# Attention rows normalised by the product that transposes them

## The chip, the cores and the metric

The kernel runs on one core of a Trainium2 chip. The metric is the device time of one execution in microseconds (us). Before the change it is 1858.86 us, the median of three runs (1857.93 to 1861.39).

TensorE multiplies: `matmul(out, a, b)` writes aᵀ·b to PSUM, with `a` loaded as weights and `b` streamed through. VectorE, ScalarE and GpSimd work on tiles of 128 partitions, and SyncE issues most transfers.

## The reference, cut to what matters

The network is a two-layer block (a sparse attention, a gated linear attention, two MLPs), followed by a second block (attention, a two-way mLSTM, a gated FFN). All is in f32. Two of its parts take a softmax over keys and multiply the result by values:

```python
# layer A: 16 heads, 4 key heads, 512 tokens, causal, best 128 keys a query
logits = einsum('bqgrd,bqkgd->bqgrk', q_b, k_sel) * 64 ** -0.5
p = softmax(where(valid, logits, -inf), axis=-1)
o = einsum('bqgrk,bqkgd->bqgrd', p, v_sel)
...
# second block: 8 heads, 2 key heads, 512 tokens, no mask
s = einsum('bkgqd,bksd->bkgqs', q_blk, kt) * 64 ** -0.5
p = softmax(s, axis=-1)
o = einsum('bkgqs,bksd->bkgqd', p, vt)
```

## The kernel before, in words

Weights are cut into a high and a low part (type f32r) and each projection is made of three f32r products per block (`wh` by `xT_hi`, `wh` by `xT_lo`, `wl` by `xT_hi`); these are the rows named `ps_a` at line 77. Plain f32 products, not cut, are used in a few places: values of the attentions, the memory heads (lines 1241 and 1275), the gated linear attention (line 786 and others).

`softmax_pv` (line 410) does one block of 128 queries for eight heads. For each head:

1. Two f32r products give the scores in a PSUM bank of tag `s` (two banks). The queries carry a minus sign, so that the row minimum `mn` stands for the maximum.
2. VectorE takes the row minimum (line 428 with a mask, line 431 without).
3. ScalarE takes exp into `prob` and sums the row into `sum` (line 434).
4. VectorE takes the reciprocal `rcp` (line 436).
5. The tile `prob` is multiplied by `rcp` in place, on VectorE (line 438) or ScalarE (line 440), as a letter of `norm` says for each of the four heads of a group: `"dada"` in layer A, `"addd"` in the second block (`d` is VectorE, `a` is ScalarE).
6. TensorE transposes `prob` in pieces of 128 columns into a bank of tag `t` (two banks, line 443). The piece is the weights, the identity `net.ident` is streamed.
7. The bank is copied to `pt` (line 446 on VectorE, line 448 on ScalarE).

When four heads of a group are done, plain f32 products of values and `pt` follow (tag `o`).

Layer A calls it eight times: four query blocks with 1, 2, 3 and 4 key blocks of 128 (`W` = 128 to 512), and two groups of eight heads each. The second block calls it four times, always with `W` = 512. That is 96 heads and 288 transposes.

Around the attentions a list of steps (`ORDER_A`, `ORDER_2`) puts projections beside them, and a scheduler then sets the order on each engine by its own estimate of every instruction's cost, so that projection products stand between those of the attention. Each engine works through its own queue in order.

Of the kernel before, what the change touches and what calls it, by code (L numbers as in the profile page):

```python
# [10 lines left out]
F32 = mybir.dt.float32  # L11
F32R = mybir.dt.float32r
I32 = mybir.dt.int32
AF = mybir.ActivationFunctionType
ALU = mybir.AluOpType
# [11 lines left out]
P = 128  # L27
# [382 lines left out]
def softmax_pv(net, pool, t, W, nkb, qT, kTh, kTl, v, g0, bias, oh, ol, kofs, pw=512, norm="addd", copy="dddd"):  # L410

    nc = net.nc
    tsl = slice(t * P, (t + 1) * P)
    pso = net.bank("o")
    pts = []
    for gi in range(2):
        pt = pool.tile([P, NT, 4, P], F32, name="pt", bufs=2)
        for r in range(4):  # L420
            h = 4 * gi + r
            ps = net.bank("s")
            net.mm(ps[:, :W], qT[:, h, tsl], kTh[:, g0 + gi, :W], True, False)
            net.mm(ps[:, :W], qT[:, h, tsl], kTl[:, g0 + gi, :W], False, True)
            mn = pool.tile([P, 1], F32, name="mn", bufs=4)
            pr = pool.tile([P, pw], F32, tag="prob", name="prob", bufs=4)[:, :W]
            if bias is not None:
                nc.vector.tensor_tensor_reduce(pr, ps[:, :W], bias, 1.0, 3.0e38, ALU.add, ALU.min, mn)
                src = pr
            else:  # L430
                nc.vector.tensor_reduce(mn, ps[:, :W], axis=AX.X, op=ALU.min)
                src = ps[:, :W]
            sm = pool.tile([P, 1], F32, name="sum", bufs=4)
            nc.scalar.activation(pr, src, AF.Exp, bias=mn, scale=-1.0, accum_out=sm)  # L434
            rc = pool.tile([P, 1], F32, name="rcp", bufs=4)
            nc.vector.reciprocal(rc, sm)
            if norm[r] == "d":
                nc.vector.tensor_scalar(pr, pr, rc, None, op0=ALU.mult)
            else:
                nc.scalar.activation(pr, pr, AF.Copy, scale=rc)  # L440
            pst = net.bank("t")
            for kb in range(nkb):
                nc.tensor.transpose(pst[:, kb * P : (kb + 1) * P], pr[:, kb * P : (kb + 1) * P], net.ident)  # L443
            ptv = pst[:, :W].rearrange("p (k n) -> p k n", k=nkb)
            if copy[r] == "d":
                nc.vector.tensor_copy(pt[:, :nkb, r, :], ptv)
            else:
                nc.scalar.activation(pt[:, :nkb, r, :], ptv, AF.Copy)
        pts.append(pt)

    for kb in range(nkb):
        for gi in range(2):
            net.mm(pso[gi * 64 : gi * 64 + 64, :], v[:, kb, g0 + gi, :], pts[gi][:, kb].rearrange("p r n -> p (r n)"), kb == 0, kb == nkb - 1)
    net.split(oh[:, kofs : kofs + 4, tsl], ol[:, kofs : kofs + 4, tsl], pso.rearrange("p (r n) -> p r n", r=4))


def layer_a(net, first):
# [3 lines left out]
    with tc.tile_pool(name="da", bufs=1) as da:  # L461
# [8 lines left out]
        with tc.tile_pool(name="di", bufs=1) as di, tc.tile_pool(name="dr", bufs=2) as dr:  # L470
# [67 lines left out]
            def attend(t, gp):  # L538
                if gp == 0 and "oa" not in have:
                    have["oa"] = da.tile([P, 2, 4, S], F32R, tag="iq", name="oa")  # L540
                oh, ol = (have["oa"][:, 0], have["oa"][:, 1]) if gp == 0 else (net.xh, net.xl)
                softmax_pv(net, di, t, (t + 1) * P, t + 1, qT[gp], kTh, kTl, v, 2 * gp, bias[t], oh, ol, 4 * gp, 576, "dada", "aaaa")
# [462 lines left out]
def second(net):  # L1005
# [5 lines left out]
    with tc.tile_pool(name="sm", bufs=1) as sm:  # L1011
# [8 lines left out]
        with tc.tile_pool(name="sa", bufs=1) as sa:  # L1020
# [80 lines left out]
            with tc.tile_pool(name="sp2", bufs=1) as sp2:  # L1101
                run_steps(ORDER_2[1], flows, {"A": lambda t: softmax_pv(net, sp2, t, S, NT, qT, kTh, kTl, v, 0, None, oah, oal, 0)})
# [420 lines left out]
```

## Time and profile before

| what | value |
|---|---|
| median of three runs | 1858.86 us |
| profiled execution, its own time | 1859.66 us |
| its span, first to last instruction | 1857.9 us |
| mean granted TensorE clock | 0.993 |
| TensorE busy | 1815.5 us (98%) |
| VectorE busy | 1440.5 us (78%) |
| ScalarE busy | 912.3 us (49%) |
| TensorE products | 10564 |

PE is TensorE, PEld its weight loads, DVE is VectorE, ACT ScalarE, POOL GpSimd. Busy time is what an engine spent in instructions; several of TensorE's overlap, since products are pipelined, so the pace of a run of equal products is read from the run's length less one product's length, over their number less one. A granted clock of 1.00 is 2.4 GHz, one of 0.50 is 1.2 GHz. The chain of waits goes back from the last instruction to what released it at every step: only what stands on it sets the end.

### The profile page before, as it was taken

What the parts mean: (1) busy time and instruction counts of PE and PEld (TensorE: products, weight loads), DVE (VectorE), ACT (ScalarE), POOL (GpSimd) and SP (SyncE); (2) the same over time, 40 slices, a digit from 0 to 9 for tenths busy, and PEclk for the clock granted to TensorE, in tenths of its full rate; (3) what the DMA queues carried; (4) which work ended last, traced back from release to release, by engine and by line L of the source; (5) the groups of instructions that cost most, each with busy time, mean ns of one, the idle gap of its engine ahead of it and who ended that gap; (6) DMA issues with size and microseconds to landing.
All of it is one profiled execution on the core that took longest, in us unless ns stands there. A gap on an engine that the chain in (4) does not pass through costs nothing.

```text
span 1857.9 us, 26802 instructions
## 1 busy us (share of the span) xinstructions
PE 1815.5 (98%) x10564; PEld 1532.8 (83%) x10564; DVE 1440.5 (78%) x2467; ACT 912.3 (49%) x1600; POOL 19.0 (1%) x46
## 2 busy tenths in 40 slices
PE   8999999999999999999999999999999899999997
PEld 7865698988888888889888888777566689999996
DVE  5998589878678587468988777877876787788877
ACT  5568644444443544334544444445677445344334
POOL 0010000000000100000000000000000000000000
PEclk9999999999999999999999999999999999999999
DMA  4231244634324222126454323422112122333232
GB/s 143 91 68 52 67 139 158 207 117 148 103 91 134 61 69 69 68 91 188 140 180 140 113 92 111 139 73 81 46 41 69 45 91 68 114 114 114 79 104 91
DMA packets 127161, 190.80 MB, mean 103 GB/s; under 512 B 9279, under 2 KB 77835, under 8 KB 127036
## 3 DMA queue, kind: packets, MB, share of 16 engines
q1 hardware_dynamic: 126996, 189.03, 32.0%
q8 instruction: 83, 1.36, 0.3%
q14 instruction: 42, 0.34, 0.1%
q0 software_dynamic: 32, 0.07, 0.0%
q10 hardware_dynamic: 8, 0.00, 0.0%
HBM read 186.96 MB, written 2.12 MB: 102 GB/s over the span
## 4 chain that ended last, share of the span: by engine, by line
PE 92%; DVE 5%; ACT 2%; issue 0%; DMA 0%; POOL 0%; SPq 0%; DVEq 0%; ACTq 0%; POOLq 0%
PE ps_a L77 51%; PE ps_s L77 15%; PE ps_t L77 11%; PE ps_o L77 7%; PE ps_t L443 1%; PE ps_t L302 1%; PE ps_s L806 1%; PE ps_a L1275 1%; DVE wl L85 1%; PE ps_t L405 1%; PE ps_s L1241 1%; ACT prob L434 0%; PE ps_s L843 0%; PE ps_o L858 0%; ACT wh L88 0%
## 5 line engine op out<-in xcount | busy, mean ns | idle before, releaser
L88 ACT ACTIVATE wh<-wr 128x1024 fp32r<-128x1024 f32 (+2 forms) x284 | 258.6, 958 | 239.3 <-PE ps_t L77 113.3
L85 DVE TENSOR_TENSOR wl<-wr,wh 128x1024 fp32r<-128x1024 f32 (+2 forms) x284 | 304.1, 1104 | 84.6 <-ACT wh L88 55.1
L77 PE MATMUL ps_a<-wh,xT_hi 128*128 128x512 f32 (+3 forms) x536 | 205.3, 387 | 3.6 <-ACT xT_hi L88 2.2
L77 PE MATMUL ps_a<-wh,xT_lo 128*128 128x512 f32 (+3 forms) x536 | 204.3, 385 | 0.6 <-DVE xT_lo L85 0.6
L88 ACT ACTIVATE wsh<-wr 128x1024 fp32r<-128x1024 f32 x94 | 97.5, 1059 | 184.3 <-DVE wr L254 155.5
L77 PE MATMUL ps_a<-xT_hi,wh 128*128 128x256 f32 (+1 forms) x528 | 163.4, 321 | 0.9 <-DVE gtok L1097 0.5
L77 PE MATMUL ps_a<-xT_lo,wh 128*128 128x256 f32 (+1 forms) x528 | 162.7, 319 | 0.0
L77 PE MATMUL ps_a<-xT_hi,wl 128*128 128x256 f32 (+1 forms) x528 | 147.0, 319 | 0.0
L77 PE MATMUL ps_a<-wl,xT_hi 128*128 128x512 f32 (+3 forms) x536 | 143.6, 381 | 0.0
L77 PE MATMUL ps_s<-wh,hh 128*128 128x512 f32 x344 | 136.6, 397 | 0.1
L77 PE MATMUL ps_s<-wh,hl 128*128 128x512 f32 x344 | 136.7, 397 | 0.0
L77 PE MATMUL ps_a<-tl,wsh 128*128 128x256 f32 x528 | 132.1, 283 | 0.0
L77 PE MATMUL ps_a<-th,wsh 128*128 128x256 f32 x528 | 132.1, 282 | 0.0
L77 PEld LDWEIGHTS ps_a<-wh,xT_hi 128*128 128x128 f32 x536 | 101.5, 189 | 25.0 <-issue 4.5
L85 DVE TENSOR_TENSOR wsl<-wr,wsh 128x1024 fp32r<-128x1024 f32 x94 | 113.0, 1221 | 10.7 <-ACT wsh L88 10.7
L77 PEld LDWEIGHTS ps_a<-wh,xT_lo 128*128 128x128 f32 x536 | 101.5, 189 | 19.8 <-DVE xT_lo L85 1.4
L77 PE MATMUL ps_t<-wh,hl 128*128 128x512 f32 x296 | 117.4, 397 | 0.0
L77 PE MATMUL ps_t<-wh,hh 128*128 128x512 f32 x296 | 117.4, 396 | 0.0
L77 PEld LDWEIGHTS ps_a<-wl,xT_hi 128*128 128x128 f32 x536 | 95.6, 188 | 19.3 <-issue 1.6
L77 PEld LDWEIGHTS ps_a<-xT_hi,wh 128*128 128x128 f32 x528 | 100.1, 190 | 9.3 <-issue 0.8
L77 PEld LDWEIGHTS ps_a<-xT_lo,wh 128*128 128x128 f32 x528 | 100.0, 189 | 7.8 <-issue 0.8
L77 PEld LDWEIGHTS ps_a<-tl,wsh 128*128 128x128 f32 x528 | 100.3, 190 | 0.0
(437 smaller groups left out, 4122.3 us busy)
## 6 DMA issues: line engine op xcount, KB each, us to landing
wr<-in_mlp_w_up_dram SPq DMA_DIRECT2D x32, 1024.0 KB
wr<-in_mlp_w_down_dram SPq DMA_DIRECT2D x32, 1024.0 KB
mod_raw<-in_w_ada_dram SPq DMA_DIRECT2D x48, 512.0 KB
wr<-in_b_w_in_dram SPq DMA_DIRECT2D x12, 1024.0 KB
wr<-in_w_gate_dram SPq DMA_DIRECT2D x11, 1024.0 KB
wr<-in_w_up_dram SPq DMA_DIRECT2D x11, 1024.0 KB
wr<-in_w_in_dram SPq DMA_DIRECT2D x10, 1024.0 KB
wr<-in_w_down_dram SPq DMA_DIRECT2D x10, 1024.0 KB
```

The source lines that it names most:

```text
L77: self.nc.tensor.matmul(ps, lt, rt, start=first, stop=last)
L85: (eng or self.nc.vector).tensor_tensor(out, x, hi.bitcast(F32), op=ALU.subtract)
L88: self.nc.scalar.activation(out, x, AF.Copy)
L302: self.nc.tensor.transpose(ps[:, j * P : (j + 1) * P], src[:, j * P : (j + 1) * P], self.ident)
L405: nc.tensor.transpose(ps[:, j * P : (j + 1) * P], st[:, j0 + j, :], net.identr)
L443: nc.tensor.transpose(pst[:, kb * P : (kb + 1) * P], pr[:, kb * P : (kb + 1) * P], net.ident)
L806: nc.tensor.matmul(ps[:, c * 64 : c * 64 + 64], x[:, c * C : (c + 1) * C], xv[:, c * m : (c + 1) * m, 1, :], start=True, stop=True)
L1241: nc.tensor.matmul(ps, qk[:, 4 + h, a * P : (a + 1) * P], qk[:, h, :], start=True, stop=True)
L1275: nc.tensor.matmul(o, ws[a][:, b * P : (b + 1) * P], v1[:, a, h, 0:129], start=n == 0, stop=n == len(as_) - 1)
```

## The change

For each head a new tile `diag` of 128x128 is made: the identity, scaled row by row by `rcp`, on the engine that scaled `prob` before. `prob` stays unscaled. In place of the transposes stand matrix products of the same pieces of `prob` (weights) with `diag` (streamed), so that the result is probᵀ times the diagonal of reciprocal sums.

```diff
@@ -434,13 +434,15 @@
             nc.scalar.activation(pr, src, AF.Exp, bias=mn, scale=-1.0, accum_out=sm)
             rc = pool.tile([P, 1], F32, name="rcp", bufs=4)
             nc.vector.reciprocal(rc, sm)
+
+            dg = pool.tile([P, P], F32, name="diag", bufs=3)
             if norm[r] == "d":
-                nc.vector.tensor_scalar(pr, pr, rc, None, op0=ALU.mult)
+                nc.vector.tensor_scalar(dg, net.ident, rc, None, op0=ALU.mult)
             else:
-                nc.scalar.activation(pr, pr, AF.Copy, scale=rc)
+                nc.scalar.activation(dg, net.ident, AF.Copy, scale=rc)
             pst = net.bank("t")
             for kb in range(nkb):
-                nc.tensor.transpose(pst[:, kb * P : (kb + 1) * P], pr[:, kb * P : (kb + 1) * P], net.ident)
+                nc.tensor.matmul(pst[:, kb * P : (kb + 1) * P], pr[:, kb * P : (kb + 1) * P], dg, start=True, stop=True)
             ptv = pst[:, :W].rearrange("p (k n) -> p k n", k=nkb)
             if copy[r] == "d":
                 nc.vector.tensor_copy(pt[:, :nkb, r, :], ptv)
```

The scheduler sees other costs, and the order on the engines moves inside the two attentions. After the change the products of line 443 are at line 445.

TensorE, layer A, third query block of the second head group (`qT_171`, `W` = 384), before: scores `ps_s`, transposes `ps_t`, values `ps_o`, projection `ps_a`.

```order
L77 MATMUL ps_s<-kTh,qT_171 128x384
L77 MATMUL ps_s<-kTl,qT_171 128x384
L443 MATMUL ps_t<-ident,prob 128x128 x4
L77 MATMUL ps_s<-kTh,qT_171 128x384
L77 MATMUL ps_s<-kTl,qT_171 128x384
L77 MATMUL ps_o<-pt,v 64x512 x7
L443 MATMUL ps_t<-ident,prob 128x128 x6
L77 MATMUL ps_a<-wh,oa 128x512
L77 MATMUL ps_a<-wh,xT_hi 128x512
L443 MATMUL ps_t<-ident,prob 128x128 x6
```

The same place after the change:

```order
L77 MATMUL ps_a<-wh,oa 128x512 x3
L77 MATMUL ps_o<-pt,v 64x512 x7
L445 MATMUL ps_t<-diag,prob 128x128 x12
L77 MATMUL ps_s<-kTh,qT_171 128x384
L77 MATMUL ps_s<-kTl,qT_171 128x384
L77 MATMUL ps_s<-kTh,qT_171 128x384
L77 MATMUL ps_s<-kTl,qT_171 128x384
L77 MATMUL ps_o<-pt,v 64x512
L77 MATMUL ps_s<-kTh,qT_171 128x384
```

Twelve products to `ps_t` that stood in two runs of six, with projection products between, now stand in one, and three of the projection products stand ahead of them.

TensorE, second block, first query block (`aqT` are its queries), the difference; lines with - are of the kernel before, lines with + of the changed one.

```order
 L77 MATMUL ps_s<-akTh,aqT 128x512
 L77 MATMUL ps_s<-akTl,aqT 128x512
-L443 MATMUL ps_t<-ident,prob 128x128 x8
+L77 MATMUL ps_a<-xT_hi,wh 128x512
+L77 MATMUL ps_a<-xT_lo,wh 128x512
+L77 MATMUL ps_a<-xT_hi,wl 128x512
+L77 MATMUL ps_a<-xT_hi,wh 128x512
+L77 MATMUL ps_a<-xT_lo,wh 128x512
+L445 MATMUL ps_t<-diag,prob 128x128 x8
+L77 MATMUL ps_a<-xT_hi,wl 128x512
```

Here five projection products moved in ahead of the eight. Counted from the first to the last product to `ps_t` of an attention, projection products of 512 columns fall from 127 to 104 in layer A and from 119 to 104 in the second block. Outside the two attentions TensorE's order is the same, and so are the orders of SyncE's and GpSimd's queues.

## Rows read from the trace of the kernel before

**Rows 1.** The page: busy us (share of the span) xinstructions of each engine
```profile
span 1857.9 us, 26802 instructions
PE 1815.5 (98%) x10564; PEld 1532.8 (83%) x10564; DVE 1440.5 (78%) x2467; ACT 912.3 (49%) x1600; POOL 19.0 (1%) x46
```

**Rows 2.** Busy time by stretch: layer A's attention, between, second block's attention
```profile
core 0: us, PE busy (x) PEld busy (x) DVE busy (x) ACT busy (x) POOL busy (x), PEclk, DMA share, GB/s
...
105.00:216.00 111.00, 104.36 (x524) 67.58 (x524) 89.49 (x324) 94.32 (x259) 6.37 (x16) 1.00 0.18 48
216.00:1300.00 1084.00, 1076.00 (x6262) 928.93 (x6263) 831.78 (x1232) 479.07 (x727) 11.57 (x22) 1.00 0.37 117
1300.00:1386.00 86.00, 81.48 (x389) 55.04 (x389) 75.31 (x152) 60.64 (x107) 0.00 (x0) 0.98 0.15 37
```

**Rows 3.** Chain of waits, 105 to 216 us: shares by line
```profile
by line: PE ps_a L77 22.5%; PE ps_o L77 19.8%; PE ps_t L443 13.9%; PE ps_s L77 13.8%; ACT prob L434 6.4%; DVE prob L428 3.7%; ACT pt L448 3.0%; issue 2.1%; PE ps_t L405 1.9%; ACT prob L440 1.9%; DVE m L533 1.6%; ACT wh L88 1.3%; DVE sc L534
```

**Rows 4.** Chain of waits, 1300 to 1390 us: shares; pieces (start, us, what)
```profile
by line: PE ps_a L77 37.5%; PE ps_o L77 21.9%; PE ps_t L443 12.1%; PE ps_s L77 11.4%; DVE pt L446 5.6%; DVE mn L431 3.5%; DVE prob L438 2.7%; DVE wl L85 2.6%; ACT prob L434 1.8%; issue 0.7%; DVE rcp L436 0.5%
...
1318.50 3.58 PE ps_o L77 x14
...
1338.45 4.99 PE ps_o L77 x14
1359.68 2.33 PE ps_a L77 x10
```

**Rows 5.** Instructions of line 443: duration ns min/median/max, first and last start, forms
```profile
L443 PE MATMUL ps_t<-ident,prob x288: 270/272/332, 109.8 to 1384.1; 128*128 128x128 f32 x144
```

**Rows 6.** Timeline, second block: start us, us, engine, line, operation (one run of eight)
```profile
1306.25 1.03 PE L443 MATMUL ps_t<-ident,prob 128*128 128x128 f32 x8
```

**Rows 7.** Instructions of line 1275
```profile
L1275 PE MATMUL ps_a<-mv,wexp x160: 273/275/422, 1409.1 to 1460.2; 128*128 128x129 f32 x160
```

**Rows 8.** Instructions of lines 1241 and 786
```profile
L1241 PE MATMUL ps_s<-mqk x32: 590/592/697, 1399.9 to 1448.1; 128*128 128x512 f32 x32
...
L786 PE MATMUL ps_s<-ones,kq x32: 164/250/258, 655.4 to 710.0; 128*128 128x1 f32 x32
```

**Rows 9.** Timeline: runs of plain f32 products
```profile
655.41 0.95 PE L786 MATMUL ps_s<-ones,kq 128*128 128x1 f32 x8
...
1421.60 2.40 PE L1275 MATMUL ps_a<-mv,wexp 128*128 128x129 f32 x20
...
1437.05 1.02 PE L1241 MATMUL ps_s<-mqk 128*128 128x512 f32 x2
...
1456.10 0.71 PE L1275 MATMUL ps_a<-mv,wexp 128*128 128x129 f32 x4 [1.55 <-DVE wexp L1264]
```

**Rows 10.** Groups by shape, scalings: count, busy us, mean ns, idle before
```profile
L438 DVE TENSOR_SCALAR prob<-prob,rcp 128x512 f32<-128x512 f32 x32 | 15.1, 479 | 0.2
L438 DVE TENSOR_SCALAR prob<-prob,rcp 128x128 f32<-128x128 f32 x8 | 2.4, 304 | 0.0
...
L440 ACT ACTIVATE prob<-prob,rcp 128x512 f32<-128x512 f32 x16 | 11.5, 719 | 3.6 <-DVE rcp L436 3.5
L440 ACT ACTIVATE prob<-prob,rcp 128x128 f32<-128x128 f32 x8 | 3.2, 398 | 1.0 <-DVE rcp L436 1.0
```

**Rows 11.** Waits of TensorE, both attentions: us in total, times, longest
```profile
PE ps_s L77 <- DVE mn L428: 2.3, 6, 0.8
...
PE ps_s L77 <- ACT qT L407: 1.1, 1, 1.1
...
PE ps_t L443 <- DVE prob L438: 2.0, 2, 1.2
...
PE ps_s L77 <- ACT prob L434: 1.2, 3, 0.9
```

**Rows 12.** Busy time by stretch: the gap at 1334 us
```profile
1334.00:1338.00 4.00, 2.26 (x12) 1.24 (x11) 4.00 (x6) 3.09 (x5) 0.00 (x0) 0.97 0.00 0
1338.00:1342.00 4.00, 3.55 (x12) 1.12 (x13) 4.00 (x10) 2.06 (x5) 0.00 (x0) 0.60 0.70 181
```

## The prediction

> **What bounds the kernel now.** I read the engine shares first. TensorE is busy 98% of the span, VectorE 78%, ScalarE 49% [rows 1]. Then I cut the span at the two places where `softmax_pv` runs: attention of layer A at 105 to 216 us, attention of the second block at 1300 to 1386 us. In them TensorE is idle 111.00 - 104.36 = 6.64 us and 86.00 - 81.48 = 4.52 us, together 11.2 us; the long stretch between them has 8 us in 1084 [rows 2]. VectorE and ScalarE are not idle there (89 and 94 us of 111, 75 and 61 of 86), but neither is full. The chain of waits confirms it: in the first stretch the four TensorE products by name hold 22.5 + 19.8 + 13.9 + 13.8%, the transposes of line 443 alone 13.9%, while the scaling on ScalarE (line 440) holds 1.9%; in the second, transposes 12.1% and the scaling on VectorE (line 438) 2.7% [rows 3, 4]. So a microsecond put on TensorE here is a microsecond on the end, less what falls into those 11.2 us; a microsecond taken from the scaling is worth almost nothing.
>
> **The product in place of the transpose.** The change removes 288 transposes and adds 288 products of the same shape, 128 columns through 128x128 weights. The question is what a plain f32 product costs beside an f32 transpose. The trace has 288 transposes for the 288 that the code issues (8 heads x (1+2+3+4) blocks x 2 head groups, plus 8 heads x 4 x 4): one instruction each, 272 ns long and pipelined [rows 5]. Eight of them take 1.03 us, so one follows the other by (1.03 - 0.272) / 7 = 0.108 us [rows 6].
>
> The nearest plain f32 product is the memory head's `ws` by `v1`, 129 columns, line 1275. The code issues 80 of them (8 calls x 10), and the trace has 160; line 1241 issues 16, and the trace has 32 [rows 7, 8]. A plain f32 product is two instructions with a weight load each, a transpose is one. Twenty of them (ten products) take 2.40 us [rows 9]: (2.40 - 0.275) / 19 = 0.112 us each, 0.224 a product. Added per product: 0.224 - 0.108 = 0.115 us (from unrounded spacings 0.1118 and 0.1083); times 288: **33.2 us** of TensorE.
>
> No row shows this very product, so I bound it. Below: one-column f32 products, where only the weight load is left, follow each other by (0.95 - 0.250) / 7 = 0.100 us [rows 8, 9]; two of them less one transpose is 0.092, times 288 = 26.4 us. Above: four instructions alone with a wait ahead take 0.71 us [rows 9], (0.71 - 0.275) / 3 = 0.145; two less a transpose is 0.182, times 288 = 52.3 us. I take 33.2, since the x20 row has the shape of the new work to within a column and nearly all transposes stand in runs of four or eight.
>
> The trace also says why the price doubles: at 512 columns two instructions of line 1241 take 1.02 us [rows 9], (1.02 - 0.592 [rows 8]) = 0.43 us apart, four times the 0.108 us for four times the columns. An f32 instruction goes at one rate, transpose or not, and the product needs two.
>
> The Trainium skill speaks against this change: "Perfetto Trace Analysis", section Transposes, asks that a logical transpose use the transpose and not a standard matmul, because it skips the arithmetic. The rows agree in sign, with 0.108 against 0.224 us. It gives no figure; by it alone the sum would only be known to be above zero.
>
> **The scaling.** VectorE did 56 of the 96 scalings, ScalarE 40 (by the `norm` letters: 32 and 32 in layer A, 24 and 8 in the second block). Each now scales a 128x128 identity instead of a 128xW tile. On VectorE 128x512 takes 479 ns and 128x128 304; on ScalarE 719 and 398 [rows 10]. At most 56 x 0.175 = 9.8 us leaves VectorE and 40 x 0.321 = 12.8 us ScalarE (less in truth, since 64 of the scalings are layer A's and three quarters of those are narrower than 512). TensorE's work hides nearly all of it already. What lies on the chain is 1.9% of 111 = 2.1 us and 2.7% of 90 (the chain was read from 1300 to 1390) = 2.4 us [rows 3, 4]; cut in the ratio of the durations that is 2.1 x (1 - 398/719) + 2.4 x (1 - 304/479) = 0.9 + 0.9 = 1.8 us, which I count inside the idle term, not beside it.
>
> **The idle term.** TensorE waited for the row minimum, the scaling, the exp that frees a score bank, and new queries [rows 11]. With 288 products slower TensorE asks later for each of these, and the scaling comes sooner. The others set the pace less, so idle shrinks: below, nothing of it goes; above, all 11.2 us. I take half: **-5.6 us**. A dependent part is the clock. After the gap at 1334 to 1338 us (TensorE busy 2.26 of 4) the granted clock is 0.60 in the next 4 us, between the levels 1.2 and 2.4 GHz [rows 12], and fourteen `pt` products took 4.99 us, against 3.58 elsewhere [rows 4]. If the gap closes, 1.4 us come back; I take half, **-0.7 us**.
>
> **What the new order moves.** The planner knows that the product is longer and reorders both attentions; DMA and GpSimd queues keep their order, and so does TensorE outside the attentions. Between the first and the last transposing product there stand now 104 projection products of 512 columns where there were 127 (layer A), and 104 where there were 119 (second block). They are the work that covers the waits for exp. 38 fewer at 0.233 us (ten in 2.33 us [rows 4]) are 8.9 us of cover that now stands behind the attention. Cost between zero and 8.9 us of new idle; I take zero, because the longer products themselves (4 x 0.115 us more a head of width 512) give the other engines the same time. The new tile has three buffers, so a scaling waits until the products three heads back are done; queued behind it on its engine are the next minimum or exp. At a head every 86/32 = 2.7 us in the second block and 0.9 us of products a head I expect no wait; one that came would cost at most those 0.9 us.
>
> **Sum.** The profiled execution took 1859.66 us, 0.8 above the median 1858.86. 1859.66 + 33.2 - 5.6 - 0.7 = 1886.6, on the median's footing 1885.8; I say **1886 us**. All low ends together: 1858.9 + 26.4 - 11.2 - 1.4 = 1872.7. All high ends: 1858.9 + 52.3 + 8.9 = 1920.
>
> **Rivals.**
> Starved order: the cover that moved behind the attentions is missed, idle does not shrink but grows by 8.9: 1858.9 + 33.2 + 8.9 = 1901. For it: ScalarE is busy 94 us of 111 in layer A, and the new order puts twelve products and then three score pairs with little between them. Against: its own load falls. Chance 0.10.
> Absorbed: the product goes at the weight-load pace and all idle is filled, 1858.9 + 26.4 - 11.2 = 1874. For it: the spacing hardly depends on the columns below 129 (0.100 at one). Against: waits for `mn` and `qT` remain. Chance 0.07.
> Not slower: the two instructions of a product overlap as if one, so it costs what the transpose does, and the shorter scaling gives its 1.8 us back: 1857. It decides once a product stays under 0.108 + (11.2 + 1.8) / 288 = 0.153 us. For it: weight loads overlap products in the trace. Against: no plain f32 row is below 2 x 0.100. Chance 0.03. This is also the case in which the change does not do to TensorE what it says, a matrix product with all its passes.
> Four times: an f32 product costs four transposes: 4 x 0.108 = 0.433, so 0.325 x 288 = 93.6, 1952 us. Against: [rows 9] have the ratio at two. Chance 0.02. The Trainium skill has this rule: "TensorE: Matmul & The Clock Gate", section Terms, calls the transpose mode four times faster for FP32. The trace does not bear that ratio out at this size.
>
> **How the numbers follow.** The forecast, 1876 to 1897 with its own bounds, has 0.78. The range takes it whole but for its edges, with a little of Absorbed and of Starved: 1876 to 1898. A difference within 0.2% (3.7 us) is about what a measurement of this kernel cannot tell from none. Slower holds the forecast, Starved, Absorbed and Four times: 0.97; the 0.03 of Not slower I split 0.02 faster, 0.01 same.
>
> **What would show it.** In the profile after: line 445 with 576 instructions of about 275 ns, runs of eight products spaced 0.112 us; TensorE's busy time up by some 30 us and its count from 10564 to 10852; `diag` scalings of about 300 and 400 ns; idle in the two stretches under 11.2 us and granted clock near 1 there. Line 445 with 288 instructions, or runs at 0.14 us and more, would break the price; idle above 15 us the idle term; a change of the stretch between the attentions would mean something that I have not seen.

## The result

| | before | after |
|---|---|---|
| median | 1858.39 us (1856.33 to 1861.39) | 1879.68 us (1877.19 to 1881.01) |
| ratio, 95% interval | | 1.011, [1.0098, 1.0123] |
| profiled execution, its own time | 1859.66 us | 1879.21 us |
| span | 1857.9 us | 1877.4 us |

The change makes the kernel 21 us slower (18 to 23 by the interval). The forecast was 1886, 1876 to 1898.

The page of the changed kernel, its span and the busy time of each engine, stands against [rows 1]:

```profile
span 1877.4 us, 27426 instructions
PE 1843.6 (98%) x10852; PEld 1567.6 (83%) x10852; DVE 1436.0 (76%) x2467; ACT 907.0 (48%) x1600; POOL 18.9 (1%) x46
```

TensorE has the 288 more instructions that the text spoke of, and 28 us more busy time; VectorE and ScalarE together lost 10. The line of the product, as [rows 5]:

```profile
L445 PE MATMUL ps_t<-diag,prob x576: 270/275/377, 110.1 to 1399.0; 128*128 128x128 f32 x192
```

Two instructions a product, 275 ns long. Their pace, from the timeline of the second block, as [rows 6] and [rows 9]:

```profile
1316.33 1.95 PE L445 MATMUL ps_t<-diag,prob 128*128 128x128 f32 x16
```

(1.95 - 0.275) / 15 = 0.112 us, the figure taken for the sum. Now the stages. The view of busy time by stretch, cut at the same work in both kernels (first score product of layer A to the first product of the MLP's down projection; start of the gate transposes to the first memory head), before:

```profile
97.00:287.00 190.00, 183.21 (x978) 133.54 (x977) 151.47 (x424) 124.90 (x307) 6.37 (x16) 1.00 0.32 94
1284.20:1399.90 115.70, 111.00 (x518) 75.89 (x519) 93.82 (x186) 73.22 (x123) 2.29 (x12) 0.99 0.20 56
```

and after (columns as in [rows 2]), with the long stretch between the attentions in the middle:

```profile
97.38:298.10 200.72, 198.96 (x1138) 153.79 (x1136) 150.21 (x424) 122.17 (x307) 6.26 (x16) 1.00 0.31 90
226.00:1310.00 1084.00, 1076.32 (x6263) 929.94 (x6260) 831.62 (x1232) 478.59 (x726) 11.57 (x22) 1.00 0.37 118
1294.75:1418.78 124.03, 123.84 (x646) 91.19 (x647) 91.62 (x186) 70.82 (x123) 2.29 (x12) 1.00 0.18 51
```

The two stages are 10.7 and 8.3 us longer, and that is all but half a microsecond of the difference of the spans (19.5); between them, shifted by 10 us, 1084 us hold the same work as in [rows 2] (6263 products against 6262, busy 1076.32 us against 1076.00). TensorE's idle time in the stages goes from 6.79 + 4.70 = 11.5 us to 1.76 + 0.19 = 1.95. The granted clock of the second is 1.00 where it was 0.99. The chain of waits there, against [rows 4]:

```profile
by line: PE ps_a L77 34.7%; PE ps_t L445 31.2%; PE ps_o L77 19.1%; PE ps_s L77 15.1%
...
1331.10 3.58 PE ps_o L77 x14
...
1354.84 3.58 PE ps_o L77 x14
...
1381.49 3.58 PE ps_o L77 x14
...
1400.24 3.58 PE ps_o L77 x14
```

Nothing but TensorE is left on it: the copies, minima and scalings of VectorE that held 12% of it before are gone. All four runs of fourteen value products take 3.58 us; the one of 4.99 has gone with the gap ahead of it.

The scalings, against [rows 10] (groups by shape):

```profile
L440 DVE TENSOR_SCALAR diag<-ident,rcp 128x128 f32<-128x128 f32 x56 | 15.7, 283 | 0.6
L442 ACT ACTIVATE diag<-ident,rcp 128x128 f32<-128x128 f32 x40 | 15.7, 395 | 3.5 <-DVE rcp L436 3.2
```

And what TensorE waits for in layer A's attention, 105 to 226 us, against [rows 11]; in the second block the view is empty:

```profile
PE ps_t L405 <- DVE hst L395: 0.6, 1, 0.6
PE ps_t L445 <- DVE diag L440: 0.3, 1, 0.3
PE ps_o L77 <- ACT pt L450: 0.3, 1, 0.3
PE ps_s L77 <- DVE mn L428: 0.2, 1, 0.2
```

### The profile page after: what moved, and what is told of

It reads as the page before. It is cut to its first block, busy times and chain, and to the rows that moved or that the text cites. A ratio compares the mean times of both kernels' runs of the same rounds, so it can differ in the third digit from the quotient of the medians.

```text
span 1877.4 us, 27426 instructions
## 1 busy us (share of the span) xinstructions
PE 1843.6 (98%) x10852; PEld 1567.6 (83%) x10852; DVE 1436.0 (76%) x2467; ACT 907.0 (48%) x1600; POOL 18.9 (1%) x46
## 4 chain that ended last, share of the span: by engine, by line
PE 92%; DVE 5%; ACT 1%; DMA 1%; issue 0%; POOL 0%; SPq 0%; DVEq 0%; ACTq 0%; POOLq 0%
PE ps_a L77 50%; PE ps_s L77 15%; PE ps_t L77 11%; PE ps_o L77 7%; PE ps_t L445 3%; PE ps_t L302 1%; PE ps_s L808 1%; PE ps_a L1277 1%; DVE wl L85 1%; PE ps_t L405 1%; PE ps_s L1243 1%; PE ps_s L845 0%; DMA wr<-in_w_down_dram 0%; DVE sc L536 0%; PE ps_o L860 0%
## 5 line engine op out<-in xcount | busy, mean ns | idle before, releaser
L85 DVE TENSOR_TENSOR wsl<-wr,wsh 128x1024 fp32r<-128x1024 f32 x94 | 113.0, 1220 | 12.6 <-ACT wsh L88 12.6
L77 PEld LDWEIGHTS ps_a<-wh,xT_lo 128*128 128x128 f32 x536 | 101.7, 190 | 21.1 <-DVE xT_lo L85 1.7
```

Of the source, the lines that this page charges most:

```text
L77: self.nc.tensor.matmul(ps, lt, rt, start=first, stop=last)
L85: (eng or self.nc.vector).tensor_tensor(out, x, hi.bitcast(F32), op=ALU.subtract)
```

## The experiments

Differences below are medians against the kernel before in the same group of runs, with the 95% interval of the ratio turned into us. "Stage" is the length between the marks named above, from start times in the trace; where a new order moves work across a mark, the text says so.

**The change once more, beside the next three.** No edit.

> The change itself again, beside the other kernels of this group. Every theory: +21 us over the kernel before (1.010 to 1.012). Two instructions per product, spaced 0.112 us; TensorE idle in the two attentions below 3 us together, where it was 11.2.

Measured: 1879.45 against 1857.87, +21.6 (17.6 to 23.2). It repeats.

**The product without the shorter scaling.**

```diff
 nc.vector.tensor_scalar(pr, pr, rc, None, op0=ALU.mult)   # as before
...
-nc.tensor.transpose(pst[:, kb * P : (kb + 1) * P], pr[:, kb * P : (kb + 1) * P], net.ident)
+nc.tensor.matmul(pst[:, kb * P : (kb + 1) * P], pr[:, kb * P : (kb + 1) * P], net.ident, start=True, stop=True)
```

> The scaling of the rows stays as it was before (in place, full width), only the transposes become matrix products, with the plain identity. Theory (price less stalls): the product costs 33 us on TensorE and 12 of them fall into stalls that TensorE had anyway, whatever the scaling does; so +20 to +24 us, like the whole change, idle again below 4 us. Rival 1 (scaling): those 12 us came from the shorter scaling, so without it the full price shows, +31 to +34 us. Rival 2 (order): they came from the order that the planner chose for the change; this kernel has another one (116 and 91 projection products between the first and the last product to ps_t, against 104 and 104), so the time moves away from +21 by several us either way.

Measured: 1881.89, +24.0 (20.6 to 26.9), at the upper edge of the theory's figure. Stages 201.2 and 124.6 us, beside 200.9 and 124.0 with the diagonal. So the stalls take up the product's price without any help from the scaling, and with this other order too. By the medians of the two the shorter scaling is worth 2.4 us beside the product; in the traces, 2.9 us apart, only 0.9 stand in the two stages and 2.2 behind them, where both kernels do the same.

**The shorter scaling without the product.**

```diff
-nc.tensor.matmul(pst[:, kb * P : (kb + 1) * P], pr[:, kb * P : (kb + 1) * P], dg, start=True, stop=True)
+nc.tensor.transpose(pst[:, kb * P : (kb + 1) * P], pr[:, kb * P : (kb + 1) * P], net.ident)
```

> The diagonal is made (128x128 scaling on the same engines), but the transposes stay, with the identity: rows are left unnormalised, so this is only the shorter scaling without the product. Theory: the scaling is hidden by TensorE, 0 to -3 us against the kernel before, idle of TensorE in the two attentions still 8 us and more. Rival 1 (scaling): -10 to -12 us.

Measured: 1848.38, -9.5 (-11.9 to -7.1). My figure was wrong, in its idle time too (2.6 + 1.0 us in the two stages, where I had 8 and more), and the rival's was nearly met: -10 lies inside the interval. But the edit does two things: the scaling is shorter, and the transposes no longer wait for it. The next two take these apart.

**Short, and waited for.**

```diff
-nc.vector.tensor_scalar(pr, pr, rc, None, op0=ALU.mult)
+nc.vector.tensor_scalar(pr[:, :P], pr[:, :P], rc, None, op0=ALU.mult)
...
-nc.scalar.activation(pr, pr, AF.Copy, scale=rc)
+nc.scalar.activation(pr[:, :P], pr[:, :P], AF.Copy, scale=rc)
```

> The kernel before with its transposes, but the in-place scaling covers only the first 128 columns (the other key blocks stay unnormalised): the transposes still wait for the scaling, which is as short as that of the diagonal. The run with the diagonal beside the old transposes gained 9.5 us, more than my theory had (0 to -3); there the transposes waited for exp alone, not for a scaling. Theory A (wait): those 9.5 us come from the transposes no longer standing behind reciprocal and scaling; here they still do, so 0 to -3 us. Theory B (width): they come from the 9.8 and 12.8 us less work on VectorE and ScalarE; then this kernel gains the same, -8 to -10.

Measured: 1855.57 against 1859.67, -4.1 (-5.2 to -2.0 by the ratio's interval).

**Long, and not waited for.**

```diff
+px = pool.tile([P, pw], F32, name="scaled", bufs=2)[:, :W]
-nc.vector.tensor_scalar(pr, pr, rc, None, op0=ALU.mult)
+nc.vector.tensor_scalar(px, pr, rc, None, op0=ALU.mult)
...
-nc.scalar.activation(pr, pr, AF.Copy, scale=rc)
+nc.scalar.activation(px, pr, AF.Copy, scale=rc)
```

> The kernel before with its transposes of unscaled rows; the full-width scaling is still done on the same engines, but into a tile that nobody reads (rows stay unnormalised). Theory A (wait): the transposes wait for exp alone, so -6 to -10 us although VectorE and ScalarE do all their old work. Theory B (width): 0 to -2.

Measured: 1860.55 against 1859.67, +0.9 (0.2 to 3.5). Both theories fail as put: short alone gives 4 of the 9.5 us, without the wait alone nothing, both together all. In the traces layer A's stage is 4.8 to 5.9 us shorter in all three kernels. The second block's is 5.8 us shorter where both were done and 0.4 where the scaling was only short. Where only the wait was dropped it is as long as before (115.7 us), but the last fourteen value products, 3.58 us at the usual pace, stand behind the mark there; with what follows, that kernel takes 2.5 us more than the kernel before from the start of this stage to its last instruction. Busy time by stretch, 1284 to 1392 us, of the kernel with both:

```profile
1284.00:1392.00 108.00, 107.14 (x508) 73.99 (x506) 85.38 (x181) 73.47 (x127) 2.29 (x12) 1.00 0.19 51
```

and of the one that only dropped the wait, with what TensorE waited for from 1285 to 1392 us:

```profile
1284.00:1392.00 108.00, 100.67 (x476) 70.62 (x475) 87.78 (x173) 76.03 (x123) 2.28 (x12) 0.99 0.19 53
```

```profile
PE ps_t L444 <- ACT prob L434: 5.1, 4, 2.0
PE ps_o L77 <- DVE pt L447: 0.5, 1, 0.5
```

Idle is 0.86 in the one and 7.33 in the other. Full-width scalings that nobody waits for still stand in ScalarE's and VectorE's queues, and the exp and minima of later heads come late instead: the wait for the scaling became one for exp. (The wait for exp is in the rows; that the queued scalings make exp late is argued from the order of the queues.) By the count of projection products among the second block's transposes (171 and 176) the orders of these two are alike. In the kernel before (119) and the short one (113) they are not, and no run here parts the order from the scaling there. The traced execution of the kernel that only dropped the wait (1857.17 us) is the fastest of its twelve, so its trace shows less loss than its median.

**The product's price by itself.**

```diff
+for _ in range(2):
     nc.tensor.matmul(pst[:, kb * P : (kb + 1) * P], pr[:, kb * P : (kb + 1) * P], dg, start=True, stop=True)
```

> Every product with the diagonal is issued twice into the same place. Theory: no stall is left to take it, so the second set shows at its full price, 288 x 0.224 = 64.5 us less at most 2: +83 to +87 us over the kernel before, +62 to +65 over the change. If products overlapped with their neighbours, or other engines still set the pace for a part, it would be clearly below +55 over the change.

Measured: 1945.45, +66.0 over the change and +87.6 over the kernel before. 66.0 / 288 = 0.229 us a product, just above the range given (62 to 65 us for all). With no stalls left, all of a product shows.

**One transpose more a head; all transposes twice.**

```diff
-nc.tensor.transpose(...)
+for _ in range(2 if kb == 0 else 1):
+    nc.tensor.transpose(...)
```

> The kernel before, and the first 128 columns of each head transposed twice into the same place: 96 transposes more, 96 x 0.108 = 10.4 us more on TensorE, scaling untouched. Theory (stalls of 11 to 14 us in the two attentions take the first work that comes): most of it vanishes, 0 to +4 us. Rival (a fixed share of what is added is hidden, as 21 of 33 showed with the change): +6.5 us. Rival (nothing hidden unless the scaling is shorter): +10.

Measured: 1863.37 against 1859.39, +4.0 (2.0 to 5.6), for 10.4 us of work. That is the upper edge of the theory's 0 to 4; the fixed share (6.5) and the full price (10) lie outside the interval. By stage the theory holds in layer A alone, where the stage is 0.3 us longer for 6.9 us of work. The second block's is 3.3 us longer for 3.5 us of work, with 4.24 us of idle time left in it; busy time by stretch, against the line from 1284.20 of the kernel before:

```profile
1285.49:1404.51 119.02, 114.78 (x550) 80.38 (x551) 94.22 (x186) 67.26 (x118) 2.28 (x12) 0.99 0.21 55
```

Its order there is another (69 projection products among the transposes, 119 before), and no run parts the order from the small addition. So it is not shown that stalls take the first work that comes, whichever stage it stands in.

The second has `range(2)` throughout.

> The kernel before, with all 288 transposes issued twice: 288 x 0.108 = 31.2 us more on TensorE, nearly the price of the change (33.2), scaling untouched. Theory: 9 to 12 us of it fall into stalls, +19 to +22 us, as with the product by the identity (+24). Rival (a product is dear beyond its spacing on TensorE, for its weight loads or because it cannot be reordered): well below, +10 to +15. Rival (scaling): +31.

Measured: 1877.57, +18.2 (16.4 to 21.6), for 31.2 us of work; 18.2 lies just below the theory's 19 to 22, the interval reaches into it. So 13.0 us of it vanish, with transposes that scale nothing: what the stalls take up is no property of the product. Here both stages give: 7.2 us in layer A and 6.5 in the second block, by their lengths in the trace, with 2.1 and 0.2 us of idle time left. Of the first 10.4 us added 6.4 vanish, of the next 20.8 another 6.6.

**Half the change.** `new` is `bias is None` in the first and `bias is not None` in the second.

```diff
+new = bias is None
+dg = pool.tile([P, P], F32, name="diag", bufs=3) if new else pr
+sc = net.ident if new else pr
...
+if new:
     nc.tensor.matmul(pst[:, kb * P : (kb + 1) * P], pr[:, kb * P : (kb + 1) * P], dg, start=True, stop=True)
+else:
+    nc.tensor.transpose(pst[:, kb * P : (kb + 1) * P], pr[:, kb * P : (kb + 1) * P], net.ident)
```

> The change in the second block's attention alone; layer A as before. Theory (price less stalls, stage by stage): the second block's stage was 8.3 us longer in the trace of the change, so +7 to +10 us. If the time came from somewhere else than the stage itself (clock, later stages), it would not add up with the other half to 21.

> The change in layer A's attention alone. Theory: layer A's stage was 10.9 us longer in the trace of the change, so +10 to +13 us, and with the second half +21.

Measured: 1868.71 and 1871.15 against 1859.39, +9.3 (7.8 to 12.6) and +11.8 (10.4 to 15.2). They add to 21.1; each stage keeps its own loss. The second of the two also has the second block as it was before, with 4.70 us of idle time again, but not the fall of the clock behind the gap:

```profile
1296.41:1410.83 114.42, 109.72 (x519) 75.67 (x520) 94.01 (x186) 73.21 (x123) 2.28 (x12) 1.00 0.21 57
```

The stage is 1.3 us shorter for it than in the kernel before (granted clock 0.99 there). So the clock's loss in that gap is real, but not every execution with the gap has it.

**One instruction a piece: f32r.** The first transposes scaled rows rounded to f32r, the second multiplies rounded rows by a rounded diagonal.

```diff
+prr = pool.tile([P, pw], F32R, tag="probr", name="probr", bufs=2)[:, :W]
-nc.vector.tensor_scalar(pr, pr, rc, None, op0=ALU.mult)
+nc.vector.tensor_scalar(prr, pr, rc, None, op0=ALU.mult)
...
-nc.tensor.transpose(pst[:, kb * P : (kb + 1) * P], pr[:, kb * P : (kb + 1) * P], net.ident)
+nc.tensor.transpose(pst[:, kb * P : (kb + 1) * P], prr[:, kb * P : (kb + 1) * P], net.identr)
```

> The kernel before with the scaled rows written as f32r into another tile and transposed as f32r (rounds the probabilities). The trace of the kernel before has f32r transposes of this shape 0.079 us apart (eight in 0.80 us), f32 ones 0.108: 288 x 0.029 = 8.4 us less on TensorE. Theory: part of it turns into stalls, since TensorE then asks earlier: -3 to -8 us. If the instruction count alone set the price (one as before), 0.

Measured: 1861.61 against 1859.67, no difference (ratio 0.9998 to 1.0015). The pace came as foreseen, in the timeline of the second block:

```profile
1308.21 0.80 PE L444 MATMUL ps_t<-identr,probr 128*128 128x128 f32 x8
```

(0.80 - 0.248) / 7 = 0.079 us. The 8.4 us went back in busy time by stretch:

```profile
98.00:287.00 189.00, 182.37 (x975) 132.65 (x975) 150.18 (x423) 124.78 (x306) 6.20 (x16) 0.97 0.32 93
1285.00:1370.00 85.00, 78.68 (x379) 50.68 (x378) 74.72 (x158) 50.22 (x97) 2.28 (x12) 0.96 0.13 38
```

TensorE is idle for 6.6 and 6.3 us, and the granted clock is 0.97 and 0.96 where it was 1.00 and 0.99. (The order is another here: the first memory head starts at 1371 us, before the last transposes, so the length of the second stage can't be compared.) One place in layer A, in the same view:

```profile
170.00:174.00 4.00, 2.77 (x18) 1.97 (x16) 3.55 (x8) 1.97 (x4) 0.00 (x0) 1.00 0.00 0
174.00:178.00 4.00, 2.84 (x6) 1.58 (x7) 3.32 (x11) 2.40 (x7) 0.00 (x0) 0.67 0.00 0
```

TensorE is busy 2.77 of 4 us, and in the next 4 the mean clock is 0.67, so it was at the lower of its two levels for a part. The shares say where the 8.4 us went: the clock lost 0.03 of 189 and 0.04 of 85 us, some 7 us more than before, and idle time grew by 1.4. One of the eleven executions has a mean clock of 0.994, where the others have 0.990 and 0.991; it took 1855.48 us, 4.2 less than the kernel before and inside the forecast, which fits. The edit has a side effect too: the rounded rows stand in two buffers, where the rows had four. In layer A VectorE's scaling waits 6.4 us for transposes to free one, about what its masked minimum waited for the rows' buffers before (7.6 us). Whether more buffers would have kept the gain was not run.

For the product the diagonal and exp's output are f32r:

```diff
-nc.scalar.activation(pr, src, AF.Exp, bias=mn, scale=-1.0, accum_out=sm)
+nc.scalar.activation(prr, src, AF.Exp, bias=mn, scale=-1.0, accum_out=sm)
...
-dg = pool.tile([P, P], F32, name="diag", bufs=3)
+dg = pool.tile([P, P], F32R, name="diag", bufs=3)
```

> The change with exp and the diagonal written as f32r (rounds both): one instruction per product instead of two. At the pace of the f32r transposes (0.079 us) TensorE has 8.4 us less than in the kernel before and 42 less than in the change. Theory (the number of instructions and their pace set the price; stalls take a part back): -5 to -10 us against the kernel before. If a product were dear for being a product and not for being f32: +10 us and more.

Measured: 1871.44, +11.8 (9.5 to 15.2), outside the theory's figure. One instruction a product, but slower than an f32r transpose:

```profile
1315.91 1.00 PE L446 MATMUL ps_t<-diag,probr 128*128 128x128 f32 x8
...
1333.24 1.11 PE L446 MATMUL ps_t<-diag,probr 128*128 128x128 f32 x8
```

(1.00 - 0.275) / 7 = 0.104 us, or 0.119 in the second, so it costs what an f32 transpose does. That accounts for a gain that did not come, not for 12 us of loss. In layer A, whose stage is 7.4 us longer, TensorE's idle time is 7.9 us, where it was 6.8, and it waited for the diagonal (3.2 us) and for the copies of the transposed pieces (2.0). One such gap, in busy time by stretch:

```profile
176.00:180.00 4.00, 2.80 (x17) 2.12 (x16) 1.80 (x9) 3.77 (x11) 0.00 (x0) 0.87 0.00 0
180.00:184.00 4.00, 4.00 (x11) 2.21 (x10) 1.38 (x6) 3.36 (x9) 0.00 (x0) 0.50 0.35 88
184.00:188.00 4.00, 3.80 (x19) 3.05 (x20) 1.99 (x7) 2.20 (x6) 0.00 (x0) 0.77 0.99 374
```

TensorE is busy 2.80 of 4 us, and then the granted clock is 0.50, the 1.2 GHz level, for 4 us. Over the three lines the clock lost 0.13 + 0.50 + 0.23 of 4 us, 3.4 us. The rest of the loss stays open. The product's type is not the only thing that differs: exp's output has three buffers, where it had four, and the order is another.

None of the versions that compute the attention beats the kernel before.

## Why the prediction was right, and which step was off

**What bounds the kernel** held. TensorE's extra work ended up on the end of the kernel, in the two stages and nowhere else.

**The product's price** held: two instructions, 0.112 us apart, 33.2 us. Doubling it (0.229 a product) gives 66.0 us against 64.5 worked out from that spacing. One reading behind it was off: not nearly all transposes stand in runs of four or eight, but 200 of the 288, and layer A has many shorter runs; the pace after the change came out the same. Of the two places of the Trainium skill, "Perfetto Trace Analysis", section Transposes, was right in sign (0.108 against 0.224 us). "TensorE: Matmul & The Clock Gate", section Terms, has four times for FP32; the 288 products came as 576 instructions and 2.06 times the transpose's spacing, and the measurement decides.

**The idle term and the clock** were the step that was mis-sized. I gave back 5.6 us of idle and 0.7 of clock. Against the span's +19.5 the 33.2 leave 13.7 us to be given back, and the rows have: idle 11.49 to 1.95, 9.5 us; the fourteen value products, 4.99 to 3.58, 1.4 us; and a rest of 2.8 us. The stages' busy time says the same: it grew by (198.96 - 183.21) + (123.84 - 111.00) = 28.6 us and not by 33.2. The mistake was to halve the idle time and the clock: with the whole of both, my sum would have been 1858.9 + 33.2 - 11.2 - 1.4 = 1879.5, beside 1879.68 measured. What TensorE waited for were minima, exps and scalings of the next heads, and those heads all gained the time of the longer products; that this is why nearly all of it went is my reading. That it goes without any change in the scaling is shown by the product with the identity and by the transposes issued twice, where 13.0 us vanished too.

The rest is not in the view of idle time, and its size hangs on the pair of executions: by the medians (+21.3) 11.9 us are given back, and after idle time and clock 1.0 is left. One cost that the view doesn't list is seen in score pairs of the kernel before, from the timeline:

```profile
1304.62 0.39 PE L77 MATMUL ps_s<-akTh,aqT 128*128 128x512 f32 x1
1304.85 0.39 PE L77 MATMUL ps_s<-akTl,aqT 128*128 128x512 f32 x1
...
1311.14 0.50 PE L77 MATMUL ps_s<-akTh,aqT 128*128 128x512 f32 x1 [0.18 <-ACT prob L434]
1311.48 0.40 PE L77 MATMUL ps_s<-akTl,aqT 128*128 128x512 f32 x1
```

The second of a pair follows after 0.23 us, and after 0.34 where the first had waited; the 0.11 us stand in no idle time. All three pairs of the second block that start after a wait have 0.34, whether the wait was 0.18 or 0.85 us. But pairs directly behind transposes have 0.32 without any wait, so fewer waits are only one candidate for the rest, and that they make it up is not shown.

**The scaling** was called worth almost nothing. Beside the product it is nearly that: 2.4 us. For the kernel before the statement was too weak: a shorter scaling with the wait gave 4 us, and shorter and without the wait 9.5. I had priced only what lay on the chain of waits (1.8 us) and not the stalls and the clock that hang on it. It did not hurt the forecast, since beside the product the shorter scaling found few stalls left to close; that the two draw on the same stalls is argued from the times (product alone +24.0, the shorter scaling without the product -9.5, both +21.6).

**The new order** cost nothing, as taken: idle fell though 38 projection products moved behind the attentions. The three diagonal buffers made no wait: TensorE waits 0.3 us for a diagonal in layer A.

**The rivals.** Starved order, Not slower and Four times are out by the traces (idle 1.95 us, 576 instructions, 0.112 us). Absorbed named the right place, all idle filled, with the wrong price for the product; its 1874 is 6 below the result, the forecast 6 above, so the two times alone do not tell them apart; the pace of the products does.

## What to carry to other kernels

Folding a scale into a transpose by multiplying with a diagonal turns one TensorE instruction into two in f32; count the instructions of a like product in the trace before doing it where TensorE is the bound. Work added to the engine that bounds a stage can fall into that engine's own stalls and win back the clock that they cost. Here, with about 31 to 33 us added, three times the idle time, nearly all of it was filled, so the whole listed idle time is the better term, not a half; with 10.4 us added 6.4 vanished, and one of the two stages took none. Once the stalls were gone, added work showed at its full price. In reverse, 8.4 us taken off that engine brought nothing; in the trace most of it went into a lower clock.

## What the runs showed of the hardware

An f32r product of 128 columns goes at 0.104 to 0.119 us, an f32r transpose of the same shape at 0.079, an f32 transpose at 0.108 and an f32 product at 0.224. I had expected the f32r product at the transpose's pace. And 8.4 us less work on TensorE came to nothing: in that kernel the granted clock fell to 0.97 and 0.96 in the two stretches.
